# Attention scores as two float32r products over stacked 128-row operands, in a two-block transformer step on one core

## The chip, the cores and the metric

The kernel runs on one core of one Trainium2 chip. The metric is device time in microseconds of one execution; the times given are of several runs, of which the median counts. Lower is better. One execution was also taken by the profiler, and the rows below are of that one.

## The reference, cut to what matters

The input is a sequence of 512 tokens with 1024 features. Block one is run first (two layers), then block two (two layers). A layer of block one normalises `x`, multiplies it by a large input matrix, and cuts the result into three mixers: a sliding-window attention, a forgetting attention and a state-space scan. The scores of both attentions are what changes:

```python
# sliding window: 8 query heads, 2 key heads, head size 64, blocks of 128 queries
scores = jnp.einsum('bnqkgd,bnskd->bnkgqs', qb, kcat).astype(jnp.float32) * (hd ** -0.5)
...
# forgetting attention: 8 heads, head size 64, causal, with a bias from cumulated gates
logits = jnp.einsum('bqhd,bkhd->bhqk', qi, k).astype(jnp.float32) * scale
logits = logits + ci[..., :, None] - c[:, :, None, :]
```

In the sliding window each query block of 128 sees its own and the previous key block (256 keys; the first block has 128), and queries and keys carry rotary positions. In the forgetting attention query block i sees the i + 1 key blocks up to its own (128, 256, 384 or 512 keys). After softmax and the product with the values, each head is multiplied by a gate `silu(g)`, and everything goes through an output matrix and is added to `x`. The layer ends with an attention to a memory. All arrays are float32.

## The kernel before, in words

**Layout.** Activations lie with features on the 128 partitions and the 512 tokens along the free axis, eight tiles of 128 x 512. A Tile program with named pools is compiled to one instruction queue per engine; the order in each queue comes from a scheduler that puts earlier program lines first among what is ready, so work written later fills the waits of work written earlier, as far as buffers allow.

**Projections.** `steps` (L506; run to its end by `gemm`, L476) makes one feature tile of 128 x 512 after the other. Its weights come by `load` (L453): a 512 KB transfer on SP's queue, a float32r copy `wh` by ScalarE (L460), the remainder `wl` by VectorE (L462). The product is three float32r matmuls for each of eight blocks of 128 rows (`mm3`, L469 to L474: hi by hi, hi by lo, lo by hi), 24 matmuls in one PSUM buffer of the pool "g", which has two. Then a callback takes the tile out of PSUM. After every second tile `aside` (L494) lets in two steps of the modulation matmuls of block two (`adaln`, L1040), once `self.side` is set (L712).

**The mixer** `mixer1` (L563) runs once per layer. The feature tiles of its input matrix are numbered: 0 and 1 to 4 values of the two attentions, 5 the two rotary key heads, 6 to 9 the rotary queries, 10 to 13 gates of the sliding window, 14 to 17 keys and 18 to 21 queries of the forgetting attention, 22 to 25 its gates, 26 to 37 the convolution's input, 38 to 45 gates of the state-space part. The order written is:

1. Tiles 0 and 1 (values: copy, four transposes, copy; `cb_v`, L586), then 5 to 9 (`cb_rope`, L600: four ScalarE copies that swap quarters, two VectorE and one GpSimd operation), then 2 to 4 (L617 to L619).
2. The gates' small rows and their softplus chain (L620 to L665).
3. The sliding window (L672 to L710): for each of four head pairs j, each half of the queries and each head a of the pair, one block: a bfloat16 matmul writes the mask over 512 columns (L680), two score matmuls add the products (L685), VectorE takes the maximum (L688), ScalarE the exponentials (L694), VectorE scales them (L701). `weigh` (L995) transposes the probabilities (L1004), copies them (L1007) and multiplies by the values (L1010). The gate tile 10 + j is made inside the loop (L708).
4. Tiles 14, 18, 15, 19 and so on, kept by one copy each (`cb_keep`, L716 to L722), gates 22 to 25 (L724), and the first quarter of the output projection (L725).
5. The forgetting attention (L726 to L743): for head pair j, query block i and head a, one block: two bfloat16 matmuls for bias and triangle mask (L734, L735), the score matmul (L736), `softmax_rows` (L976), `weigh`, and at the pair's end the product with the gate (L742), which frees the one PSUM buffer of the pool "o".
6. Convolution tiles 26 to 37 (`cb_conv`, L750; L765), the state-space scan (L766 to L834), further parts of the output projection.

The score operands of before are plain float32 tiles; head a of a pair lies on partitions 64a to 64a + 63:

```python
ten.matmul(s3[:, i2, 256 - n:], qT[j][a * 64:a * 64 + 64, i * P:(i + 1) * P],
           kT[a * 64:a * 64 + 64, k0:k0 + n], start=False, stop=i2 == 1)
...
ten.matmul(s_, kq[2 * j + 1][a * 64:a * 64 + 64, i * P:(i + 1) * P],
           kq[2 * j][a * 64:a * 64 + 64, :n], start=False, stop=True)
```

They lie, with values, gates and convolution outputs, in the pool "f2", which has 24 tiles of 128 x 512.

Of the kernel before, what the change touches and what calls it, by code (L numbers as in the profile page):

```python
# [10 lines left out]
F32R = mybir.dt.float32r  # L11
# [4 lines left out]
AF = mybir.ActivationFunctionType  # L16
OP = mybir.AluOpType
# [3 lines left out]
P = 128  # L21
# [213 lines left out]
class _K:  # L235
# [306 lines left out]
    def hilo(self, src, tag):  # L542
# [2 lines left out]
        self.nc.vector.tensor_tensor(lo, src, hi, OP.subtract)  # L545
        return hi, lo

    def tokens(self, src, nt, dst):

        pp = self.pt("t")[:, :nt * P]  # L550
        for i in range(nt):
            self.nc.tensor.transpose(pp[:, i * P:(i + 1) * P], src[:, i * P:(i + 1) * P], self.idf)
        self.nc.scalar.activation(dst, pp.rearrange("p (i d) -> p i d", i=nt), AF.Copy)
# [9 lines left out]
    def mixer1(self, l, x, ps, rb):  # L563
        nc = self.nc
        A = self.A
        ten, vec, act, pool = nc.tensor, nc.vector, nc.scalar, nc.gpsimd
        wf = A[f"w_f{l}"]
# [15 lines left out]
        hT = self.norm(x, 4, self.v(f"nmix{l}"), keep=small, rb=rb, ps=ps)  # L583
# [14 lines left out]
        qk = []  # L598

        def cb_rope(f, s, ps):  # L600
            sw = self.tl("tg", [P, 512])
            for b in range(4):
                act.activation(sw[b * 32:(b + 1) * 32], ps[(b ^ 1) * 32:(b ^ 1) * 32 + 32], AF.Copy)
            o = self.tl("f2", [P, 512])
            vec.tensor_tensor(o, ps, rope, OP.mult)
            pool.tensor_tensor(sw, sw, rops, OP.mult)
            vec.tensor_tensor(o, o, sw, OP.add)
            qk.append(o)

        def cb_gate(lst):  # L610
            def cb(f, s, ps):
                o = self.tl("f2", [P, 512])
                self.gate(ps, o)
                lst.append(o)
            return cb

        self.gemm(wf, range(2), [hT], cb_v, 1, 2)  # L617
        self.gemm(wf, range(5, 10), [hT], cb_rope)
        self.gemm(wf, range(2, 5), [hT], cb_v)  # L619
        zt = self.tl("tg", [P, 512])  # L620
        act.activation(zt, pz, AF.Copy)
        pp = self.pt("t")
# [43 lines left out]
        kT, qT = qk[0], qk[1:5]  # L666
# [5 lines left out]
        for j in range(4):  # L672
            po = self.pt("o")
            for ip in range(2):
                p2 = []
                for a in range(2):
                    hh = 2 * j + a
                    s_ = self.pt("s")
                    s3 = s_.rearrange("p (i n) -> p i n", i=2)
                    ten.matmul(s_, self.idb, self.bandb if ip else self.band0b, start=True, stop=False)  # L680
                    for i2 in range(2):
                        i = 2 * ip + i2
                        k0 = max(i - 1, 0) * P
                        n = 256 if i else P
                        ten.matmul(s3[:, i2, 256 - n:], qT[j][a * 64:a * 64 + 64, i * P:(i + 1) * P],  # L685
                                   kT[a * 64:a * 64 + 64, k0:k0 + n], start=False, stop=i2 == 1)
                    m = self.sm("mx", [P, 2])
                    vec.tensor_reduce(m, s3, AX.X, OP.max)  # L688
                    nmx = self.sm("nmx", [P, 2])
                    vec.tensor_scalar(nmx, m, -0.125, nsink[:, hh:hh + 1], OP.mult, OP.min)  # L690
                    p3 = self.tl("t", [P, 2, 256])
                    den = self.sm("den", [P, 4])
                    for i2 in range(2):
                        act.activation(p3[:, i2], s3[:, i2], AF.Exp, bias=nmx[:, i2:i2 + 1], scale=0.125,  # L694
                                       accum_out=den[:, i2:i2 + 1])
                    act.activation(den[:, 2:4], nmx, AF.Exp, bias=self.v(f"sink{l}")[:, hh:hh + 1])
                    vec.tensor_tensor(den[:, :2], den[:, :2], den[:, 2:4], OP.add)
                    rd = self.sm("rd", [P, 2])
                    vec.reciprocal(rd, den[:, :2])
                    for i2 in range(2):  # L700
                        vec.tensor_scalar(p3[:, i2], p3[:, i2], rd[:, i2:i2 + 1], None, OP.mult)  # L701
                    p2.append(p3)
                for i2 in range(2):
                    i = 2 * ip + i2
                    self.weigh(po[:, i * P:(i + 1) * P], [p[:, i2] for p in p2],
                               [(b * P, va[:, i - 1 + b]) for b in range(0 if i else 1, 2)])
            y = self.tl("t", [P, 512])
            self.gemm(wf, [10 + j], [hT], cb_gate(ga))  # L708
            vec.scalar_tensor_tensor(y, po, 0.5, ga[j], OP.mult, OP.mult)
            y0.append(self.hilo(y, "y"))  # L710
# [3 lines left out]
        kq = []  # L714

        def cb_keep(f, s, ps):  # L716
            o = self.tl("f2", [P, 512])
            act.activation(o, ps, AF.Copy)
            kq.append(o)

        for j in range(4):
            self.gemm(wf, [14 + j, 18 + j], [hT], cb_keep)  # L722
        gb, y1 = [], []
        self.gemm(wf, range(22, 26), [hT], cb_gate(gb))  # L724
        self.gemm(A[f"w_o{l}0"], range(4), [y0], self.add_to(x), 2)  # L725
        for j in range(4):  # L726
            po = self.pt("o")
            for i in range(4):
                n = (i + 1) * P
                ss = []  # L730
                for a in range(2):
                    h = 2 * j + a
                    s_ = self.pt("s")[:, :n]
                    ten.matmul(s_, self.selb[:, h:h + 1].to_broadcast([72, P]), rows[:, :n], start=True, stop=False)  # L734
                    ten.matmul(s_[:, i * P:], self.idb, self.causb, start=False, stop=False)  # L735
                    ten.matmul(s_, kq[2 * j + 1][a * 64:a * 64 + 64, i * P:(i + 1) * P],  # L736
                               kq[2 * j][a * 64:a * 64 + 64, :n], start=False, stop=True)
                    ss.append(s_)
                pr_ = self.softmax_rows(ss, n, 0.125)
                self.weigh(po[:, i * P:(i + 1) * P], pr_, [(kt * P, vb[j][:, kt]) for kt in range(i + 1)])  # L740
            y = self.tl("t", [P, 512])
            vec.scalar_tensor_tensor(y, po, 0.5, gb[j], OP.mult, OP.mult)  # L742
            y1.append(self.hilo(y, "y"))  # L743
# [24 lines left out]
        for g in range(2):  # L768
# [4 lines left out]
            for c in range(4):  # L773
# [3 lines left out]
                o = self.tl("f2", [P, 8, 64])  # L777
# [4 lines left out]
            for c in range(4):  # L782
# [7 lines left out]
                for hf in range(2):  # L790
                    pa = self.pt("s").rearrange("p (h l) -> p h l", h=4)
                    for hh in range(4):
                        h = 8 + 8 * g + 4 * hf + hh
                        ten.matmul(pa[:, hh], self.selb[:, h:h + 1].to_broadcast([72, P]), rows[:, cs],
                                   start=hh == 0, stop=hh == 3)
# [14 lines left out]
                for ft in range(4):  # L810
                    for a in range(2):
                        hh = 2 * ft + a
                        o = py[a * 64:a * 64 + 64, ft]
# [3 lines left out]
                for ft in range(4):  # L817
                    f = 4 * g + ft
# [20 lines left out]
        for f in range(8):  # L839
# [3 lines left out]
            hi, lo = self.pair("h", 512)  # L843
# [1011 lines left out]
```

## Time and profile before

| | |
|---|---|
| median of 3 runs | 3039.6 us (3034.33 to 3042.72) |
| profiled execution | 3043.31 us |
| its span, first to last instruction | 3041.3 us |
| TensorE busy | 2846.7 us, 94% |
| VectorE busy | 1493.5 us, 49% |
| ScalarE busy | 1164.2 us, 38% |
| GpSimd busy | 267.0 us, 9% |
| mean granted clock of TensorE | 0.972 of full |

PE is TensorE's matmuls, PEld its weight loads, DVE is VectorE, ACT ScalarE, POOL GpSimd, SP the queue that issues most transfers. A name such as `pss<-f,f` says what is written and read: `pss` is the PSUM pool of the scores, `psg` that of the projections. A matmul's shape is given as rows * columns of its weights, then rows x columns of what streams through. float32 and float32r both stand as f32; float32r are L472 to L474. A float32 matmul stands as two instructions. Matmuls overlap, so their durations are longer than the distance from one start to the next; it is the starts that tell what a matmul costs.

### The profile page before, as it was taken

The numbers are of one execution on the slowest core, as the hardware profiler recorded it, in microseconds if no ns is written. First come the engines' busy times: TensorE is split into PE (matmuls) and PEld (weight loads), VectorE is DVE, ScalarE is ACT, GpSimd is POOL, SyncE is SP. The second block draws the span as 40 slices with busy tenths as digits, with TensorE's granted clock in tenths as the row PEclk, the third lists the DMA queues.
The fourth block names the chain that finished last, engine by engine and source line by source line (L and its number), as shares of the span: only waits on it lengthen the run. The fifth ranks groups of instructions, "written<-read, shape, count | busy, mean of one in ns | idle before, by whom it ended". The sixth has DMA issues, their size and how long they took to land. (4 is left out here: it accounts for less than half of the span.)

```text
span 3041.3 us, 46563 instructions
## 1 busy us (share of the span) xinstructions
PE 2846.7 (94%) x18975; PEld 1936.7 (64%) x18976; DVE 1493.5 (49%) x3051; ACT 1164.2 (38%) x2410; POOL 267.0 (9%) x256
## 2 busy tenths in 40 slices
PE   8999999999999999999989999989997999997975
PEld 5676667876777677887776788733334767774321
DVE  4625696544544687626355566631114365574100
ACT  4523454442542444434345343331112463443110
POOL 0000030000000011100011011011111010001101
PEclk9999999999999999999999999989997989997998
DMA  4142325421224134431111111489984111129998
GB/s 141 56 159 81 124 95 175 160 75 56 84 97 146 57 132 147 158 120 30 61 35 32 49 38 39 188 338 368 374 317 120 58 33 53 52 65 354 410 404 302
DMA packets 97573, 439.52 MB, mean 145 GB/s; under 512 B 11216, under 2 KB 12496, under 8 KB 72784
## 3 DMA queue, kind: packets, MB, share of 16 engines
q1 hardware_dynamic: 86976, 401.09, 36.4%
q0 software_dynamic: 9520, 32.32, 4.0%
q8 instruction: 149, 2.44, 0.3%
q10 hardware_dynamic: 864, 3.15, 0.3%
q14 instruction: 64, 0.52, 0.1%
HBM read 416.40 MB, written 20.97 MB: 144 GB/s over the span
## 5 line engine op out<-in xcount | busy, mean ns | idle before, releaser
L472 PE MATMUL psg<-h,wh 128*128 128x512 f32 x1616 | 654.1, 405 | 0.7 <-DVE x L1078 0.4
L473 PE MATMUL psg<-h,wh 128*128 128x512 f32 x1616 | 648.2, 401 | 0.0
L474 PE MATMUL psg<-h,wl 128*128 128x512 f32 x1616 | 647.2, 401 | 0.0
L462 DVE TENSOR_TENSOR wl<-wr,wh 128x1024 fp32r<-128x1024 f32 (+2 forms) x272 | 338.9, 1247 | 493.9 <-ACT wh L460 482.1
L460 ACT ACTIVATE wh<-wr 128x1024 fp32r<-128x1024 f32 (+2 forms) x272 | 280.9, 1033 | 608.6 <-PE psg L473 536.0
L472 PEld LDWEIGHTS psg<-h,wh 128*128 128x128 f32 x1616 | 305.2, 189 | 94.8 <-issue 24.6
L473 PEld LDWEIGHTS psg<-h,wh 128*128 128x128 f32 x1616 | 305.2, 189 | 75.1 <-issue 14.2
L474 PEld LDWEIGHTS psg<-h,wl 128*128 128x128 f32 x1616 | 305.5, 189 | 73.8 <-issue 12.4
L1727 PE MATMUL psg<-ew,xg 128*64 128x512 f32 x832 | 222.7, 609 | 23.8 <-DMA ew<-in_eu_dram 13.1
L472 PE MATMUL psg<-y,wh 128*128 128x256 f32 (+1 forms) x560 | 181.1, 324 | 1.5 <-ACT y L448 0.8
L473 PE MATMUL psg<-y,wh 128*128 128x256 f32 (+1 forms) x560 | 180.5, 323 | 1.9 <-DVE y L449 1.9
L474 PE MATMUL psg<-y,wl 128*128 128x256 f32 (+1 forms) x560 | 178.9, 321 | 0.0
L1727 PEld LDWEIGHTS psg<-ew,xg 128*64 128x64 f32 x832 | 65.3, 139 | 156.3 <-issue 113.6
L472 PE MATMUL psg<-f,wh 128*128 128x256 f32 (+1 forms) x360 | 115.1, 321 | 4.1 <-DVE x L557 1.8
L1007 ACT ACTIVATE t<-pst 128x512 f32<-128x512 f32 (+1 forms) x134 | 70.0, 557 | 127.6 <-PE pst L1004 124.6
L472 PEld LDWEIGHTS psg<-y,wh 128*128 128x128 f32 x560 | 107.9, 193 | 14.8 <-DVE x L1078 2.1
L473 PE MATMUL psg<-f,wh 128*128 128x256 f32 (+1 forms) x360 | 114.3, 318 | 0.8 <-DVE f L1242 0.8
L473 PEld LDWEIGHTS psg<-y,wh 128*128 128x128 f32 x560 | 107.5, 193 | 11.5 <-DVE y L449 2.2
L474 PE MATMUL psg<-f,wl 128*128 128x256 f32 (+1 forms) x360 | 113.0, 314 | 0.0
L474 PEld LDWEIGHTS psg<-y,wl 128*128 128x128 f32 x560 | 107.9, 193 | 6.1 <-issue 0.6
L1754 PE MATMUL pss<-ew,hid 128*64 128x512 f32 x400 | 106.1, 597 | 2.8 <-DMA ew<-in_ed_dram 2.6
L1004 PE MATMUL pst<-const_sb,t 128*128 128x128 f32 x488 | 84.5, 284 | 4.5 <-DVE t L1232 3.3
(465 smaller groups left out, 4431.3 us busy)
## 6 DMA issues: line engine op xcount, KB each, us to landing
ew<-in_eg_dram SPq DMA_DIRECT2D x52, 1024.0 KB, 20.9
ew<-in_eu_dram SPq DMA_DIRECT2D x52, 1024.0 KB, 8.4
ew<-in_ed_dram SPq DMA_DIRECT2D x50, 1024.0 KB, 8.8
wm<-in_wm_dram SPq DMA_DIRECT2D x96, 512.0 KB, 3.8
wr<-in_w_f_dram SPq DMA_DIRECT2D x92, 512.0 KB, 3.5
wr<-in_v_f_dram SPq DMA_DIRECT2D x60, 512.0 KB, 3.3
wr<-in_w_o_dram SPq DMA_DIRECT2D x32, 512.0 KB, 3.5
x<-in_ed_dram SPq DMA_DIRECT2D x10, 1024.0 KB, 10.3
```

Source lines behind the costliest of these rows:

```text
L460: nc.scalar.activation(hi, raw, AF.Copy)
L462: nc.vector.tensor_tensor(lo, raw, hi, OP.subtract)
L472: t.matmul(ps, a[0], b[0], start=first, stop=False)
L473: t.matmul(ps, a[0], b[1], start=False, stop=False)
L474: t.matmul(ps, a[1], b[0], start=False, stop=last)
L1004: ten.transpose(pp[:, (2 * i + a) * P:(2 * i + a + 1) * P], ps[a][:, c:c + P], self.idf)
L1007: self.nc.scalar.activation(pT[:, :w], pp[:, :w], AF.Copy)
L1727: ten.matmul(ps[e * 64:(e + 1) * 64], x0[:, d, e * 64:(e + 1) * 64], wn[e][:, k], start=d == 0, stop=d == 7)
L1754: ten.matmul(ps[e * 64:(e + 1) * 64], hid[0, q][:, f, e * 64:(e + 1) * 64], w[j][e][:, f], start=f == 0, stop=f == 3)
```

## The change

Each score operand becomes a tile of 128 rows for one head. For a query it holds the float32r rounding of the head's 64 rows in one half and the remainder in the other; for a key there are two tiles, the rounding in both halves and the remainder in both halves. A score is then the sum of two float32r matmuls over 128 rows with the same query tile, one with each key tile. The rotary result goes to the pool "t" first. In the first part value and rotary tiles alternate. Half of the forgetting attention's key and query tiles (16, 20, 17, 21) and its four gates are projected inside the loop over head pairs, not ahead of it.

```diff
+    def stacked(self, src, double):
+        act, vec, pool = self.nc.scalar, self.nc.vector, self.nc.gpsimd
+        lo_, up_ = slice(0, 64), slice(64, 128)
+        if not double:
+            o = [self.tl("f2", [P, 512], F32R) for _ in range(2)]
+            for a, (m, n) in enumerate(((lo_, up_), (up_, lo_))):
+                act.activation(o[a][m], src[m], AF.Copy)
+                vec.tensor_tensor(o[a][n], src[m], o[a][m], OP.subtract)
+            return o
+        o = [[self.tl("f2", [P, 512], F32R) for _ in range(2)] for _ in range(2)]
+        for a, (m, n) in enumerate(((lo_, up_), (up_, lo_))):
+            hi, lo = o[a]
+            act.activation(hi[m], src[m], AF.Copy)
+            act.activation(hi[n], src[m], AF.Copy)
+            vec.tensor_tensor(lo[m], src[m], hi[m], OP.subtract)
+            pool.tensor_copy(lo[n], lo[m])
+        return o
+
+    def scores(self, ps, q, k, last):
+        self.nc.tensor.matmul(ps, q, k[0], start=False, stop=False)
+        self.nc.tensor.matmul(ps, q, k[1], start=False, stop=last)
...
-            o = self.tl("f2", [P, 512])
+            o = self.tl("t", [P, 512])
...
-            qk.append(o)
+            qk.append(self.stacked(o, not qk))
...
-        self.gemm(wf, range(5, 10), [hT], cb_rope)
-        self.gemm(wf, range(2, 5), [hT], cb_v)
+        self.gemm(wf, (5, 2, 6, 3, 7, 4, 8, 9), [hT], lambda f, *a: (cb_v if f < 5 else cb_rope)(f, *a))
...
-                        ten.matmul(s3[:, i2, 256 - n:], qT[j][a * 64:a * 64 + 64, i * P:(i + 1) * P],
-                                   kT[a * 64:a * 64 + 64, k0:k0 + n], start=False, stop=i2 == 1)
+                        self.scores(s3[:, i2, 256 - n:], qT[j][a][:, i * P:(i + 1) * P],
+                                    [k[:, k0:k0 + n] for k in kT[a]], i2 == 1)
...
         def cb_keep(f, s, ps):
-            o = self.tl("f2", [P, 512])
-            act.activation(o, ps, AF.Copy)
-            kq.append(o)
-
-        for j in range(4):
+            kq.append(self.stacked(ps, f < 18))
+
+        gb, y1 = [], []
+        for j in range(2):
             self.gemm(wf, [14 + j, 18 + j], [hT], cb_keep)
-        gb, y1 = [], []
-        self.gemm(wf, range(22, 26), [hT], cb_gate(gb))
         self.gemm(A[f"w_o{l}0"], range(4), [y0], self.add_to(x), 2)
...
-                    ten.matmul(s_, kq[2 * j + 1][a * 64:a * 64 + 64, i * P:(i + 1) * P],
-                               kq[2 * j][a * 64:a * 64 + 64, :n], start=False, stop=True)
+                    self.scores(s_, kq[2 * j + 1][a][:, i * P:(i + 1) * P], [k[:, :n] for k in kq[2 * j][a]], True)
...
+            if j < 2:
+                self.gemm(wf, [16 + j, 20 + j], [hT], cb_keep)
+            self.gemm(wf, [22 + j], [hT], cb_gate(gb))
             y = self.tl("t", [P, 512])
             vec.scalar_tensor_tensor(y, po, 0.5, gb[j], OP.mult, OP.mult)
```

## Rows read from the trace of the kernel before

**Rows 1.** The page, busy us (share of the span), instructions.

```profile
PE 2846.7 (94%) x18975; PEld 1936.7 (64%) x18976; DVE 1493.5 (49%) x3051; ACT 1164.2 (38%) x2410; POOL 267.0 (9%) x256
```

**Rows 2.** Busy time by stretch; last PEclk, DMA share, GB/s.

```profile
91.00:159.00 68.00, 67.85 (x397) 44.52 (x398) 46.47 (x145) 38.86 (x117) 0.00 (x0) 1.00 0.13 40
159.00:250.00 91.00, 91.00 (x475) 69.53 (x470) 25.67 (x27) 20.82 (x26) 0.00 (x0) 1.00 0.52 177
250.00:340.00 90.00, 90.00 (x511) 54.62 (x510) 56.90 (x135) 42.93 (x108) 0.51 (x5) 1.00 0.12 37
...
340.00:385.00 45.00, 44.44 (x259) 30.71 (x260) 29.81 (x46) 14.53 (x20) 0.61 (x6) 1.00 0.61 211
385.00:456.00 71.00, 66.93 (x517) 48.42 (x516) 66.99 (x134) 41.88 (x110) 24.91 (x19) 1.00 0.25 83
...
806.00:874.00 68.00, 67.85 (x389) 44.91 (x388) 46.38 (x144) 38.69 (x116) 0.00 (x0) 1.00 0.13 40
```

**Rows 3.** Waits of PEld, 43 to 456 us: total us, times, longest.

```profile
PEld pso L1010 <- ACT t L1007: 9.8, 24, 0.8
...
PEld psg L472 <- ACT wh L460: 2.5, 6, 0.4
```

**Rows 4.** Timeline of PE, two sliding-window blocks: start us, us, then the instruction.

```profile
96.94 0.39 PE L680 MATMUL pss<-cstb 128*128 128x512 bf16 x1
...
98.31 0.50 PE L473 MATMUL psg<-h,wh 128*128 128x512 f32 x1
98.65 0.40 PE L474 MATMUL psg<-h,wl 128*128 128x512 f32 x1
...
113.25 0.38 PE L680 MATMUL pss<-cstb 128*128 128x512 bf16 x1
...
114.40 0.50 PE L472 MATMUL psg<-h,wh 128*128 128x512 f32 x1
```

**Rows 5.** Timeline of PE, three blocks of the forgetting attention.

```profile
269.85 0.22 PE L735 MATMUL pss<-cstb 128*128 128x128 bf16 x1
270.00 0.49 PE L736 MATMUL pss<-f,f 64*128 64x128 f32 x2
270.42 0.50 PE L473 MATMUL psg<-h,wh 128*128 128x512 f32 x1
...
285.78 0.22 PE L735 MATMUL pss<-cstb 128*128 128x128 bf16 x1
285.93 1.12 PE L736 MATMUL pss<-f,f 64*128 64x512 f32 x2
286.98 0.39 PE L734 MATMUL pss<-rows,cstb 72*128 72x512 bf16 x1
...
296.95 0.22 PE L735 MATMUL pss<-cstb 128*128 128x128 bf16 x1
...
297.73 0.28 PE L734 MATMUL pss<-rows,cstb 72*128 72x256 bf16 x1
```

**Rows 6.** Timeline of PE, float32r projections of 512 and 256 columns.

```profile
40.01 0.39 PE L472 MATMUL psg<-h,wh 128*128 128x512 f32 x1
...
40.46 0.39 PE L474 MATMUL psg<-h,wl 128*128 128x512 f32 x1
...
560.00 0.28 PE L473 MATMUL psg<-f,wh 128*128 128x256 f32 x1
...
560.60 0.28 PE L472 MATMUL psg<-f,wh 128*128 128x256 f32 x1
```

**Rows 7.** Single lines: instructions, duration in ns min/median/max, first and last start.

```profile
L718 ACT ACTIVATE f<-psg x16: 577/582/603, 157.9 to 915.8; 128x512 f32<-128x512 f32 x16
L605 DVE TENSOR_TENSOR f<-psg,f x10: 691/692/692, 55.0 to 791.7; 128x512 f32<-128x512 f32 x10
L460 ACT ACTIVATE wh<-wr x272: 630/1059/1082, 16.9 to 2743.3; 128x1024 fp32r<-128x1024 f32 x124, 128x768 fp32r<-128x768 f32 x8, 128x512 fp32r<-128x512 f32 x4
L462 DVE TENSOR_TENSOR wl<-wr,wh x272: 682/1226/2350, 19.0 to 2744.2; 128x1024 fp32r<-128x1024 f32 x124, 128x768 fp32r<-128x768 f32 x8, 128x512 fp32r<-128x512 f32 x4
```

## What the change should do to the time

> **What bounds the kernel now.** I read first the engines' shares, then the busy times by stage, then what TensorE waits for, then the order of its instructions. TensorE is busy for 94% of the span [rows 1]. The changed code lies in the token mixer of block one, which runs once per layer. In layer 0 its stretches are the sliding-window attention (91 to 159 us), the key, query and gate projections with the first part of the output projection (159 to 250), the forgetting attention (250 to 340), the rest of the convolution projections (340 to 385) and the state-space part (385 to 456). In the first four TensorE is busy for all but 0.7 us of 294, at the full granted clock; VectorE is busy for 46.5 of 68, 25.7 of 91, 56.9 of 90 and 29.8 of 45, ScalarE for less. Only in the fifth is VectorE nearly full (67.0 of 71) [rows 2]. Layer 1 repeats this: its sliding-window stretch has the same 68 us to a tenth [rows 2]. So up to the state-space part a microsecond less of TensorE work is a microsecond less of time, as long as other matmuls are ready. They are: the instructions of a projection stand between those of the attention, one or a few at a time [rows 4, 5], so the scheduler fills the softmax's latency with projections. The waits say the same: in the 413 us from 43 to 456 TensorE's weight loads waited 2.5 us for the split weights and 9.8 us, in 24 waits, for the copies of transposed probabilities [rows 3].
>
> **What the scores cost.** A score product of before reads float32 tiles over 64 rows and is run as two passes. In the sliding window a block is one 512-column mask matmul (L680) and two products. With two of 256 columns it takes from 96.94 to 98.31, 1.37 us; the float32r projection matmul behind it needs 0.34 to its successor (98.31 to 98.65) where such matmuls otherwise follow each other at 0.225 (40.01 to 40.46 in two steps), so the change of shape costs another 0.11. With products of 128 and 256 columns it is 113.25 to 114.40, 1.15 us and the 0.11 [rows 4, 6]. In the forgetting attention, from the start of the triangle mask (L735) to the instruction behind the product: 1.20 us for 512 columns, 0.78 for 256, 0.57 for 128 [rows 5]; 384 columns lie midway between the first two, 0.99.
>
> **What they will cost.** The new product is two float32r matmuls over 128 rows (the float32 operand's rounded part in one half, its remainder in the other; the keys' rounded part twice, then their remainder twice). That is the form of the projections, which follow each other at 0.225 us for 512 columns and 0.12 for 256 (560.00 to 560.60 in five steps) [rows 6]; 384 columns midway, 0.173. No float32r matmul of 128 columns stands in the trace. It can hardly cost more than a float32 pass of 128 columns, 0.21 (270.00 to 270.42 for two) [rows 5], nor less than half of 0.12; I take 0.12, the nearest row of the same kind, since a narrower matmul should not take longer than a wider one. Before the first float32r matmul of a block I leave the 0.15 us that now pass between mask and product (285.78 to 285.93) [rows 5]; at best it is 0.06.
>
> The sums, per layer:
> Sliding window, 8 blocks of 256 and 256: 1.37 + 0.11 now, 0.225 + 4 x 0.12 = 0.705 after, 0.775 less each, 6.2 us. 8 blocks of 128 and 256: 1.15 + 0.11 now, 0.705 after, 0.555 each, 4.4 us.
> Forgetting attention, 8 blocks of each width: 512: 1.20 - (0.15 + 0.45) = 0.60; 384: 0.99 - 0.50 = 0.49; 256: 0.78 - 0.39 = 0.39; 128: 0.57 - 0.39 = 0.18; together 1.66 x 8 = 13.3 us, and the 0.11 behind every second of the 32 blocks (the others are followed by a mask, without it), 1.8 us.
> 25.7 us per layer, **51 us** for both. Ends: with 0.21 for the 32 products of 128 columns per layer 2.9 us per layer are lost, 46 in all; with 0.06 for them, and 0.06 instead of 0.15 ahead of the 32 blocks of the forgetting attention, 4.8 us per layer are won, 61.
>
> **A rule against it.** The float32r stream has each matmul with a weight load of its own, all over the same 128 rows, and yet runs at 0.225 and 0.12, so the loads are hidden behind the matmuls before [rows 6]. The Trainium skill, "TensorE: Matmul & The Clock Gate", Part 3, says that a weight load overlaps with matmuls in flight only when the row group differs; by it the old products (rows 0 to 63, then 64 to 127) would be the ones that overlap, and the new ones would not. Here the trace speaks against the rule as far as this goes: it is the 64-row product that is followed by 0.34 instead of 0.225 [rows 4].
>
> **What is added.** In ScalarE: a key tile has four half-tile copies, a query tile two; L718's plain copy goes. Per layer 4 + 8 in the rotary projections, 16 + 8 - 8 in the others: 28 copies of 512 columns at 0.58, 16 us. VectorE: two subtractions per tile, 26 per layer at 0.69, 18 us [rows 7]. GpSimd: ten half-tile copies per layer; nothing waits for them but a key tile's scores, and GpSimd does nothing in the forgetting attention's 90 us but 0.5 us [rows 2]. All of it lies beside projections: a projection tile takes TensorE 24 x 0.225 = 5.4 us, and a key tile of the second kind needs ScalarE 4 x 0.58 and 1.06 for the next weights (3.4), VectorE 2 x 0.69 and 1.23 (2.6) [rows 7]. A rotary key tile needs ScalarE for four shifted copies as well (5.7 us), over 5.4, but there is one per layer, and the new order puts value tiles between, which need 1.2 and the weights. If that cover is gone, the price is the 34 us per layer themselves. A PSUM buffer of the projections (there are two) is held for some 3 us in place of 0.6; the next tile writes the other for 5.4.
>
> **What is moved.** The order of value and rotary tiles changes no work; the value transposes stay. Key and query tiles 16, 20, 17, 21 and the gates 22 to 25, eight tiles or 43.5 us of TensorE, go from the stretch ahead of the forgetting attention into it, with their weight loads on SP's queue and the modulation matmuls that every second tile lets in. They become the fill that five of the convolution tiles are now, and these go behind; TensorE's sum is the same. The pool of 24 float tiles makes this order necessary: 4 values, 12 for two pairs, 6 for the next and a gate are 23, so convolution outputs cannot be made early. New wait: in a head pair j the product of output and gate (L742) comes after gate 22 + j, and the one PSUM buffer of the output is free only then; behind it wait the next pair's value matmuls on TensorE, while projections are ready. I cost it at nothing: the gate tile itself fills the time. VectorE in the sliding-window stretch: 46.5 us in 68 - 10.6 = 57.4, 81%; still under TensorE.
>
> For stalls that show when TensorE is quicker I take 5 us of the 51 back (a quarter of the 9.8 us of [rows 3] in each layer, an estimate). So 46 us less. The profiled execution has 3043.3 us (span 3041.3), 3.7 over the median of 3039.6; 46 from the median gives 2994.
>
> **Rivals.**
> A. *The softmax sets the sliding window's length.* VectorE has the softplus chain there too, its queue is in order, and 81% may be full in practice. Then that stretch keeps its 68 us and its 10.6 us per layer are lost: 51 - 5 - 21 = 25 less, 3015. For it: VectorE has the highest share of the first four stretches there. Against: TensorE can take key and query tiles from the stretch behind, where VectorE has 25.7 of 91 [rows 2].
> B. *Weight loads no longer hidden*, as a mechanism of these products: each of the 128 products per layer pays its load of 0.19 us, 24 of the 25.7 us, and 3 us in all are left, 3036: no change. That is what the skill's rule above would give. Against: the stream at 0.12.
> C. *The stacking becomes the bound, slower.* Copies and subtractions stand in the same in-order queues as the weight split (L460, L462) and the exponentials; once a tile's work there passes TensorE's 5.4 us, TensorE waits for split weights. All 34 us exposed against 25.7 won: 8 us per layer, 3056. It decides from the point where key tiles fall among exponentials in the forgetting attention, ScalarE 42.9 of 90 now. Against: there ScalarE has 47 and VectorE 33 of 90 us free, and five convolution tiles with four VectorE sweeps each leave it.
> D. *The products do not run as single passes*, but as the float32 ones do. Then the second product doubles the scores' passes (sliding window 16 blocks at 1.37 or 1.15 less the mask and its wait, 0.30 to 0.32, 15 us; forgetting the four widths' times less 0.15, together 2.94, by 8, 24 us), 39 us per layer, 3118. Against: the projections have the same type.
>
> **How the numbers follow.** Forecast 0.70, A 0.14, B 0.04, C 0.06, D 0.02; 0.04 is left for mixtures between A and no change. A measurement of this kernel tells 0.3%, 9 us, from no change. Forecast and A are faster, with half of the rest: 0.86; B and the other half the same: 0.06; C and D slower: 0.08. The range goes from 61 us less (2978) to A with 5 us more of stalls (3020); the forecast alone would be 2978 to 2999.
>
> **What would show it.** Right: blocks with L680 at about 0.7 us, the 512-column forgetting product 0.45 in two matmuls, no 0.34 behind; sliding-window and forgetting stretches still without TensorE idle time, everything behind them earlier by 21 to 28 us per layer; the state-space part's 71 us unchanged. Wrong: TensorE waiting for L460, L462 or for the key copies (C), VectorE near 100% from 91 to 150 us with TensorE waiting there for the scalings of L701 or the copies of L1007 (A), 0.3 us between 256-column products (B).

## The result, and the profile after

| | before | after |
|---|---|---|
| median of four runs | 3039.2 us (3034.3 to 3042.7) | 3013.4 us (3010.2 to 3019.4) |
| ratio to before | | 0.992 (0.9907 to 0.9934) |
| once more, beside the last experiments | 3038.7 | 3011.8, 0.9915 (0.9902 to 0.9929) |
| profiled execution, its span | 3043.3, 3041.3 | 3010.2, 3007.3 |
| last state-space chunk of layer 1 begins (L787, after: L810) | 1154.1 | 1124.9 |

The change makes the kernel 26 us faster; 46 were forecast. The last row of the table is where block one's changed part ends in the trace (the last start of the line, before and after):

```profile
L787 ACT ACTIVATE t<-pss x16: 255/277/278, 385.5 to 1154.1; 128x128 f32<-128x128 f32 x16
L810 ACT ACTIVATE t<-pss x16: 252/277/280, 369.2 to 1124.9; 128x128 f32<-128x128 f32 x16
```

It leaves out what follows, which took 1876 to 1887 us in the kernels below with the same code. By it the change gives 29 us, 16 in layer 0 and 13 in layer 1. It is used below beside the timed ratios. But it is read from one execution: a second one of the changed kernel has 1124.3, and 0.9 us less in layer 0, so differences of about 1 us say nothing.

The busy time by stretch, layer 0 of the changed kernel, with columns as in [rows 2] (window, its length, then PE, PEld, DVE, ACT and POOL busy, granted clock, DMA share, GB/s); the sliding window now ends at 167 us, the forgetting attention runs from 202 to 300, the state-space part from 369:

```profile
43.00:91.00 48.00, 42.49 (x195) 34.24 (x194) 18.08 (x20) 25.91 (x38) 5.09 (x5) 1.00 0.28 88
91.00:128.00 37.00, 34.12 (x190) 26.50 (x189) 27.22 (x75) 22.98 (x54) 2.57 (x2) 1.00 0.24 71
128.00:167.00 39.00, 38.76 (x268) 27.92 (x267) 29.79 (x85) 27.58 (x82) 1.22 (x2) 1.00 0.18 61
...
202.00:300.00 98.00, 97.52 (x650) 70.00 (x650) 54.48 (x125) 49.55 (x118) 2.45 (x4) 1.00 0.27 92
300.00:369.00 69.00, 69.00 (x377) 53.13 (x376) 52.25 (x76) 25.06 (x36) 1.11 (x11) 1.00 0.51 176
369.00:440.00 71.00, 66.83 (x514) 48.26 (x513) 67.26 (x135) 41.59 (x109) 24.34 (x19) 1.00 0.24 83
```

From 128 us on TensorE stands still for 0.7 us up to the state-space part, which keeps its 71 us. But from 43 to 128 us it is idle for 8.4 of 85 us. Before, the same two stretches were

```profile
43.00:91.00 48.00, 47.22 (x218) 38.37 (x218) 17.96 (x19) 25.85 (x38) 6.47 (x5) 1.00 0.33 99
91.00:128.00 37.00, 36.85 (x200) 24.20 (x198) 26.32 (x86) 20.41 (x61) 0.00 (x0) 1.00 0.14 43
```

with 0.9 us idle. So the first part of the mixer, where projections run almost alone, and the begin of the sliding window lost 7.5 us of what the attentions won. The waits of PE, 43 to 385 us, in the changed kernel (columns as in [rows 3]):

```profile
PE pst L577 <- ACT tg L613: 5.5, 4, 1.7
PE pst L648 <- ACT tg L645: 2.5, 1, 2.5
```

L577 are the transposes of a value tile (L552 before), L613 the ScalarE copy that they read; L648 transposes the gates' small rows, whose copy is L645. Before, these waits were 0.8 us in all:

```profile
PE pst L552 <- ACT tg L588: 0.8, 1, 0.8
```

The timeline shows how they come about, first all engines, 57 to 61 us:

```profile
57.56 0.63 ACT L562 ACTIVATE f<-t 64x512 fp32r<-64x512 f32 x1 [2.13 <-DVE t L632]
58.21 0.63 ACT L563 ACTIVATE f<-t 64x512 fp32r<-64x512 f32 x1
...
58.86 0.63 ACT L562 ACTIVATE f<-t 64x512 fp32r<-64x512 f32 x1
...
59.51 0.63 ACT L563 ACTIVATE f<-t 64x512 fp32r<-64x512 f32 x1
...
60.16 0.60 ACT L613 ACTIVATE tg<-psg 128x512 f32<-128x512 f32 x1
...
60.81 0.66 PE L577 MATMUL pst<-const_sb,tg 128*128 128x128 f32 x4 [1.70 <-ACT tg L613]
```

ScalarE has made the key tile's four shifted copies, waits 2.13 us for the sum of the rotation (product on VectorE, product on GpSimd, sum on VectorE), then makes the four stacking copies; the value tile's copy is the next in its queue. TensorE's last projection matmul had begun at 58.72; the transposes are its next instruction, and the projections behind them start only after them.

The score blocks, sliding window and forgetting attention of 512 columns (L704 is the mask, L570 and L571 the two products, L755 and L756 bias and triangle):

```profile
103.65 0.39 PE L704 MATMUL pss<-cstb 128*128 128x512 bf16 x1
...
104.11 0.28 PE L570 MATMUL pss<-f,f 128*128 128x256 f32 x1
104.23 0.28 PE L571 MATMUL pss<-f,f 128*128 128x256 f32 x1
104.34 0.40 PE L472 MATMUL psg<-h,wh 128*128 128x512 f32 x1
104.58 0.39 PE L473 MATMUL psg<-h,wh 128*128 128x512 f32 x1
...
242.48 0.22 PE L756 MATMUL pss<-cstb 128*128 128x128 bf16 x1
242.51 0.48 PE L570 MATMUL pss<-f,f 128*128 128x512 f32 x1
242.82 0.40 PE L571 MATMUL pss<-f,f 128*128 128x512 f32 x1
243.06 0.39 PE L755 MATMUL pss<-rows,cstb 72*128 72x512 bf16 x1
```

The first block takes 0.69 us where 1.37 stood [rows 4], the second 0.58 where 1.20 stood [rows 5], and the projection behind follows at 0.24, not 0.34.

### The profile page after: what moved, and what is told of

Its sections match the earlier page's. It is cut to its first block, busy times and chain, and to the rows that moved or that the text cites. A ratio compares the mean times of both kernels' runs of the same rounds, so it can differ in the third digit from the quotient of the medians.

```text
span 3007.3 us, 46731 instructions
## 1 busy us (share of the span) xinstructions
PE 2794.3 (93%) x18975; PEld 1932.1 (64%) x18976; DVE 1532.0 (51%) x3103; ACT 1198.2 (40%) x2466; POOL 278.6 (9%) x276
```

## The experiments

Medians with the ratio to the kernel before and its 95% interval; the third column of numbers is the begin of layer 1's last state-space chunk in the trace.

| kernel | median, us | ratio | chunk, us | at half clock |
|---|---|---|---|---|
| before | 3036.4 to 3039.2 | | 1154.1 | 0 |
| changed | 3013.4, 3011.8 | 0.992, 0.9915 | 1124.9, 1124.3 | 1, 1 |
| old order of tiles | 3008.8 | 0.9901 (0.9887 to 0.9915) | 1122.3 | 3 |
| new order alone | 3039.3 | 1.0006 (0.9996 to 1.0016) | 1154.5 | 0 |
| one product | 2985.6 | 0.9833 (0.9817 to 0.9849) | 1102.5 | 1 |
| value copy on VectorE | 3011.2 | 0.9903 (0.9887 to 0.9919) | 1123.9 | 2 |
| move alone | 3033.7 | 0.9991 (0.9981 to 1.0000) | 1146.7 | 2 |
| rotary stacking on GpSimd | 3003.4 | 0.9884 (0.9866 to 0.9902) | 1117.9 | 1 |
| the same, old order | 3001.1 | 0.9893 (0.9876 to 0.9909) | 1114.8 | 3 |
| keep copies twice | 3014.2 | 0.9922 (0.9904 to 0.9940) | 1127.0 | 2 |
| early gates | 3007.7 | 0.9896 (0.9882 to 0.9911) | 1121.5 | 1 |
| early gates, GpSimd | 3001.6 | 0.9879 (0.9863 to 0.9894) | 1118.1 | 2 |
| early gates, GpSimd, old order | 3001.0 | 0.9877 (0.9862 to 0.9892) | 1112.4 | 1 |

The traces differ in the granted clock too. Each has a stretch of 6.8 us at half the clock where layer 1 begins. The last column of the table counts the further stretches of 3.4 us at half the clock up to the last chunk (in the move alone and keep copies twice, one of the two lengthens the stretch at the begin of layer 1). In most of them TensorE is busy throughout, so such a one costs some 1.7 us, an estimate. The three of the old order:

```profile
84.80:88.20 3.40, 3.40 (x11) 2.80 (x10) 0.36 (x1) 0.60 (x1) 0.00 (x0) 0.51 0.56 154
784.60:788.00 3.40, 3.40 (x9) 2.67 (x8) 0.00 (x0) 0.13 (x1) 0.00 (x0) 0.50 0.53 154
1112.30:1115.70 3.40, 3.40 (x14) 2.02 (x14) 3.40 (x4) 0.28 (x1) 1.09 (x1) 0.50 0.40 149
```

**The order of the tiles undone.** The theory: the transposes wait because value tiles now stand between rotary ones.

```diff
-        self.gemm(wf, (5, 2, 6, 3, 7, 4, 8, 9), [hT], lambda f, *a: (cb_v if f < 5 else cb_rope)(f, *a))
+        self.gemm(wf, range(5, 10), [hT], cb_rope)
+        self.gemm(wf, range(2, 5), [hT], cb_v)
```

> The changed kernel with the first part's tiles in the old order (key and queries 5 to 9 in a row, then values 2 to 4), all else as changed. Theory: the missing 8 us per layer are TensorE's waits for value transposes and for the gates' small transposes, whose ScalarE copies stand behind the rotary and stacking copies in ScalarE's queue; then 14 us come back, 2999 us (2994 to 3004), and the waits of the value transposes fall from some 8 us per layer to under 2. Rival: with stacking, rotary tiles in a row keep ScalarE busy for 4.6 to 5.7 us of each 5.4 and hold PSUM, so TensorE waits in another place and the time stays at 3010 to 3016. Second rival: the loss is in the sliding window, which VectorE sets; then the order is worth under 4 us.

Only 2.6 us came back by the trace, and the intervals of the two ratios overlap. Two more stretches at half the clock than in the changed kernel, an estimated 3.4 us, may hide as much again. The waits of PE, 43 to 300 us, and the busy time from 43 to 167:

```profile
PE pst L577 <- ACT tg L613: 3.6, 3, 2.5
PE psg L472 <- DVE t L630: 2.7, 3, 1.2
```

```profile
43.00:167.00 124.00, 118.03 (x656) 90.56 (x654) 75.30 (x180) 74.72 (x172) 9.31 (x9) 0.99 0.25 77
```

TensorE is idle for 6.0 us instead of 8.6. The small transposes' wait is gone and the value transposes still wait 3.6 us, not under 2; a new wait stands there: projections wait for a PSUM buffer until VectorE's rotary product (L630) has read it. So the order makes a part of the loss, not the whole of it. What the trace shows is the rival's mechanism, though the time, 3008.8, lies just below the rival's 3010 to 3016.

**The new order alone**, in the kernel before (the same lines the other way round).

> The kernel before with the alternating order of value and rotary tiles alone. Theory: without stacking ScalarE has 2.4 us of rotary copies per tile, not 4.7 to 5.0, so a value tile's copy waits less; 2 to 6 us slower than before (3041 to 3046), since four shifted copies still stand ahead of each. Rival (the order is free by itself, the waits come from stacking alone): within 2 us of before.

No difference, 0.4 us in the trace; the forecast loss of 2 to 6 us did not come. Without stacking the alternation costs nothing, so the waits need the stacking copies.

**The value copy on VectorE.**

```diff
         def cb_v(f, s, ps):
             t = self.tl("tg", [P, 512])
-            act.activation(t, ps, AF.Copy)
+            vec.tensor_copy(t, ps)
```

> The changed kernel with the value tiles' copy out of PSUM on VectorE in place of ScalarE; the order of tiles is the changed one. If ScalarE's queue is what the value transposes wait for, their waits shrink from 6 us per layer to under 2 and 8 to 12 us come back (3001 to 3005 us); the gates' small transposes keep their 2.5 us per layer. If it is the pool of the copies' tiles (three, shared with the rotary part) that holds them, the waits stay and so does the time (3010 to 3016).

```profile
PE pst L577 <- DVE tg L613: 3.5, 3, 1.2
PE pst L648 <- ACT tg L645: 2.5, 1, 2.5
```

The waits fell from 5.5 to 3.5 us, not to under 2: VectorE's queue in turn holds the copy behind rotary sums and remainders. By the trace 1.0 us is won, no more than two executions of one kernel differ by; one more stretch at half the clock, an estimated 1.7 us, hides some of it. So one copy out of ScalarE's queue is not enough.

**The rotary stacking's rounded copies on GpSimd**, which has little else to do there.

```diff
+    def stacked(self, src, double, pooled=False):
...
-                act.activation(o[a][m], src[m], AF.Copy)
+                (pool.tensor_copy(o[a][m], src[m]) if pooled else act.activation(o[a][m], src[m], AF.Copy))
...
-            act.activation(hi[m], src[m], AF.Copy)
-            act.activation(hi[n], src[m], AF.Copy)
+            (pool.tensor_copy(hi[m], src[m]) if pooled else act.activation(hi[m], src[m], AF.Copy))
+            (pool.tensor_copy(hi[n], src[m]) if pooled else act.activation(hi[n], src[m], AF.Copy))
...
-            qk.append(self.stacked(o, not qk))
+            qk.append(self.stacked(o, not qk, True))
```

> The changed kernel with the rounded copies of the rotary operands made by GpSimd in place of ScalarE (12 half-tile copies per layer; order of tiles as changed, the other key and query tiles as changed). Theory: ScalarE's in-order queue is what the value transposes and the gates' small transposes wait for, and its load in the first part falls back to that of before: TensorE's idle time from 43 to 167 us falls from 8.6 us to 2 to 3, and 10 to 14 us come back in both layers, 2999 to 3003 us. Rival: it is the length of the rotary chain itself (VectorE, GpSimd, VectorE, copies) with two PSUM buffers, and GpSimd's 0.6 us copies after its 1.3 us product only lengthen it: 3010 us or more.

> The same with the tiles in the old order (5 to 9, then 2 to 4). If ScalarE's queue is the cause, the order is then worth little: 2998 to 3004 us, within 4 us of the run with GpSimd copies in the alternating order, and TensorE waits under 1 us for PSUM buffers held by the rotary product. If rotary tiles in a row are too much for the two PSUM buffers whoever copies, it stays at 3007 to 3011, where the old order alone was.

Busy time by stretch with GpSimd's copies, new order:

```profile
43.00:91.00 48.00, 47.22 (x216) 38.23 (x215) 20.29 (x22) 24.42 (x35) 14.02 (x14) 1.00 0.31 94
91.00:128.00 37.00, 33.59 (x192) 25.80 (x191) 30.46 (x86) 19.31 (x52) 5.36 (x6) 1.00 0.20 65
```

From 43 to 91 us TensorE is as full as before the change: 0.8 us idle where the changed kernel has 5.5. The wait for the value copies is 0.8 us. This is the test that settles the cause there: same order, same tiles, same stacking, only the rounded copies gone from ScalarE. What is not won back stands at the begin of the sliding window, 3.4 us in 91 to 128, now as waits for exponentials and the small rows:

```profile
PE pss L704 <- ACT t L718: 2.2, 2, 1.6
PE pst L648 <- ACT tg L645: 1.0, 1, 1.0
```

All in all 7.0 us by the trace, with as many stretches at half the clock, and 0.992 or 0.9915 against 0.9884 by the times. That is less than forecast: TensorE is idle for 4.4 us from 43 to 167, not 2 to 3, and 10 to 14 us were to come back. The old order with it gives 10.1 us by the trace, in spite of two more stretches at half the clock, and times that can't be told from these; with rotary tiles in a row there are still 2.2 us of waiting for PSUM from 43 to 167, where under 1 was expected.

**The gates' small rows and softplus chain ahead of the rotary and value tiles**: L644 to L690 of the changed kernel placed behind the first two value tiles; once with ScalarE's copies, twice with GpSimd's.

> The changed kernel with the gates' small rows and softplus chain ahead of the rotary and value tiles, ScalarE's rotary copies kept. It takes away the wait of the small transposes alone (2.5 us per layer, and in layer 1 the 3.4 us at half clock behind it, worth 1.7): 4 to 8 us less than the changed kernel, 3005 to 3010; the value transposes' waits stay at some 5.5 us per layer. If the lost time is all in the value transposes' waits: no change (within 3 us).

> The kernel with GpSimd's rotary copies (alternating order), and the gates' small rows with their softplus chain written ahead of the rotary and value tiles, not behind them. Theory: the copy that the small transposes wait for then stands ahead of the rotary copies, and some 12 us of VectorE's short operations leave the sliding window; TensorE's idle time from 43 to 167 us falls from 4.4 us to about 2, 3 to 8 us less than the run with GpSimd copies alone (2995 to 3000). Rival: the chain's own transposes and products now stop the projections while they wait for VectorE, and nothing is won (3001 to 3006).

> The same with tiles 5 to 9 in a row and 2 to 4 behind them. By the theory within 4 us of the alternating order, 2995 to 3002. If rotary tiles in a row hold PSUM too long beside the softplus chain on VectorE, 5 us or more above it.

> The changed kernel itself once more, to have it beside these on one chip: 3008 to 3016 us, 0.990 to 0.994 of before.

With ScalarE's copies 3.4 us by the trace are won (0.9896 against 0.9915, intervals overlapping): a little under the forecast. The small transposes no longer wait, but the first masks do (L704 for VectorE's L714, 2.1 us), and layer 1 keeps its 3.4 us at half the clock, from 801.8 us on; the value transposes wait 3.8 us, where 5.5 were expected to stay. With GpSimd's copies nothing is seen to be won in the new order (1118.1 against 1117.9, with one more stretch at half the clock), the rival's case. TensorE's idle time from 43 to 167 us does not fall from 4.4 to 2 but rises to 6.3, in other waits:

```profile
PE pss L704 <- ACT t L718: 2.9, 1, 2.9
PE pst L686 <- DVE parts L683: 1.1, 1, 1.1
PE pst L667 <- issue: 1.0, 1, 1.0
```

In the old order 2.4 us are won by the trace, less than the estimated 3.4 us of the two stretches at half the clock that this trace has fewer, so no gain of the early gates is shown. Of all kernels this one has the earliest chunk among those that compute everything, 12 us before the changed kernel's; by the times it is 0.9877 of before, 0.996 of the changed kernel, and not told apart from the other three with GpSimd's copies.

**One product** (the second matmul of `scores` taken out).

> The changed kernel without the second score product (the part of the scores that comes from the keys' remainder is left out). It takes TensorE work out and nothing else: per layer 24 products of 256 and 8 of 128 columns in the sliding window, 8 of each width in the forgetting attention, 3.4 and 4.6 us, 16 us for both layers. Theory, TensorE sets the time of both attentions: 13 to 17 us under the changed kernel, 2997 us. Rival, the softmax on VectorE and ScalarE sets the sliding window's length after the change: at most the forgetting attention's 9 us come, 3004 or more.

22.4 us less by the trace, 25 to 28 by the times (0.9833 against 0.9915 and 0.992; medians 2985.6 and 3013.4): more than the 16 forecast, since the second product takes 10.9 us of TensorE per layer (the sum of start-to-start distances of the score matmuls falls from 24.4 to 13.5 us), not 8. In layer 0 the chunks begin 11.8 us earlier. TensorE's work in the attentions is paid one for one: the softmax does not set the sliding window's length.

**The move alone**, in the kernel before: its `cb_keep` with one copy, tiles 16, 20, 17, 21 and 22 to 25 in the loop.

> The kernel before with the move alone: key and query tiles 16, 20, 17, 21 and the gates 22 to 25 projected inside the loop of the forgetting attention, operands and scores as before. Theory: TensorE's sum is the same and projections are ready either way, so within 3 us of before (3036 to 3042). Rival: convolution tiles that fill the attention now come behind it, where VectorE has less room, and 5 to 10 us are lost; or the new place lets more be filled and 5 to 10 are won.

The time is 2.7 us less, inside what was expected, with an interval from 0 to 5.8 us; the trace has 7.4 us, 6.6 of them in layer 0. So the move costs nothing and wins at most a few microseconds. In the trace of layer 0 the projections and modulation matmuls stand more often among their own kind; whether that is the reason was not followed up. Layer 1 has only 0.8 us of it; against it stand 6.8 us more at half the clock than before the change, an estimated 3.4 us at most.

**Keep copies twice**: in the forgetting attention's `stacked`, each ScalarE copy is issued two times.

> The changed kernel with each ScalarE copy of the forgetting attention's key and query stacking made twice (24 more copies of some 0.6 us per layer, 14 us; the result is the same). Theory: there the added work lies beside projections and costs nothing: within 3 us of the changed kernel (3010 to 3016). Rival: part of the unpaid gain is given back there too, by PSUM buffers held longer and exponentials put off; then 6 to 28 us more (3019 and up).

```profile
167.00:300.00 133.00, 132.29 (x820) 95.68 (x819) 69.65 (x143) 70.05 (x148) 3.67 (x6) 1.00 0.34 111
```

ScalarE is busy for 70.1 of these 133 us (58.7 in the changed kernel), TensorE is idle for 0.7, and the time is that of the changed kernel (in the trace 2.1 us more, with 3.4 us more at half the clock at the begin of layer 1). There the stacking is covered with room to spare.

## Why the prediction was right or wrong

**The bound** was read rightly: where attention and projections run side by side, TensorE stays full after the change, and what is taken from it is taken from the time (one product, keep copies twice).

**The range** held, but not for the reason forecast: 3013.4 us lies outside 2978 to 2999, where the forecast alone put it, and inside only because the range reached to rival A. That it came out beside A's 3015 is luck.

**The sum for the scores** was right in its mechanism, a little large. For layer 0, from 43 us to the first state-space chunk, I added up the distances from each TensorE matmul's start to the next. Scores and the three bias and mask lines go from 51.4 to 30.8 us. Transposes of probabilities go from 14.4 to 12.8; only 10 of the 136 stood directly behind a 64-row product, so most of this stays unexplained. The projections go from 237.1 to 242.9: 7.6 us more before value and small transposes, 1.8 less elsewhere, which is found behind the score products: 22 projections there cost 3.0 us over 0.225 each before, 20 cost 1.0 after. 20.6 + 1.6 + 1.8 is 24.0 us of the 25.7 predicted.

The prices of the blocks after were good (0.69 for 0.705, 0.58 for 0.60), but not their parts: the first product starts 0.03 to 0.04 us after the mask, where 0.225 and 0.15 were taken, and its second follows after 0.30 to 0.31, where 0.12 and 0.225 were taken. The two errors cancel, which is luck. The prices before were a little high, 48.5 us without the changes of shape where 46.7 are measured, for a reason not followed up. The move was put at nothing; alone, in the kernel before, it won 6.6 us in layer 0, some 5 of them in closer projections. In the changed kernel the projections that do not wait are only 1.8 us closer, and that stands behind the scores; why the two gains do not add is open.

**The step that failed** is the sentence that the added copies lie beside projections, with the one about the order of tiles: "the new order puts value tiles between, which need 1.2 and the weights". That compared ScalarE's work per tile with TensorE's 5.4 us and found it smaller. In the trace it is smaller: ScalarE is busy for 25.9 of the 48 us. But the copy that TensorE waits for stands behind a chain in an in-order queue, with ScalarE idle for 2.1 us in the middle of it. 7.6 us were lost so in layer 0, and the same four waits stand in layer 1, where I had put 2.5 per layer for all stalls. Stalls were expected in the attentions, with a quarter of [rows 3]; there hardly any came (0.7 us from 128 us on). Rival C named this mechanism, copies ahead of others in ScalarE's queue, but placed it in the forgetting attention and on the weight split, where it does not occur.

**Layer 1** lost more. There TensorE's wait for the small rows was followed by a stretch at a lower clock:

```profile
797.79 0.39 PE L474 MATMUL psg<-h,wl 128*128 128x512 f32 x1
800.70 0.84 PE L648 MATMUL pst<-const_sb,tg 128*128 128x128 f32 x4 [2.52 <-ACT tg L645]
...
801.77 0.63 PE L473 MATMUL psg<-h,wh 128*128 128x512 f32 x1
802.19 0.63 PE L474 MATMUL psg<-h,wl 128*128 128x512 f32 x1
```

```profile
801.00:804.50 3.50, 3.50 (x14) 2.70 (x13) 2.10 (x8) 2.43 (x8) 0.38 (x1) 0.51 0.31 124
```

For 3.5 us the granted clock is 0.51 of full, the level of 1.2 GHz, and projections follow each other at 0.42 us, not 0.225. That is some 1.7 us, half of the 3.4 us that layer 1 won less than layer 0; the other half was not followed up. The same stop of 2.91 us in layer 0, from the projection at 99.54 to the small transposes at 102.45, was followed by no fall of the clock.

**Rival A** gave 3015, where the time came out, but its mechanism is not what happened: from 128 to 167 us TensorE is full with VectorE at 29.8 of 39, and taking TensorE work out of the sliding window still shortens it. **Rival B** fell: the products of 128 rows follow each other at 0.12 (104.11 to 104.23 to 104.34), though each has a weight load of 0.19 us, so the loads are hidden. The rule of the Trainium skill ("TensorE: Matmul & The Clock Gate", Part 3) that the prediction set beside it, that a weight load overlaps with matmuls in flight only when the row group differs, is not borne out by this trace. **D** fell with the same rows. Stretches behind were to be earlier by 21 to 28 us per layer; they were by 16 and 13. The state-space part's 71 us came true.

What stays open: from 43 to 167 us of layer 0 TensorE was idle for 0.9 us before the change and still for 4.4, 3.5, 6.3 and 4.4 us in the four kernels with GpSimd's copies (in the order of the table), in waits that move from one place to another, some before the sliding window and some at its begin. Keeping ScalarE and VectorE clear of every rotary operation there was not tried.

## What to carry to other kernels

Work added to an engine with time to spare is free only if nothing that the bounding engine waits for stands behind it in the same queue: look in the trace at what is next in that queue, and at the chain that the added work itself waits for, before comparing sums. When a stall is found, ask whether it is the order of the work or the queue it is in; here the old order moved part of the wait to another place, and an idle engine for the copies took about half of the idle time away (8.6 to 4.4 us). A float32 product over 64 rows is worth rewriting as two float32r products over 128 where the projections around it have that form: here a pass of 256 columns fell from 0.22 us to 0.12, and most of the price of the change of shape behind it went. When two traces differ by a few microseconds, compare their granted clocks before giving the change the credit.

## What was not expected of the hardware

A float32r matmul of 128 columns, of which the trace before had none, is cheap: in blocks with no wait the first of a pair is followed by the second after 0.06 us and that by the next after 0.11.

```profile
96.80 0.22 PE L570 MATMUL pss<-f,f 128*128 128x128 f32 x1
96.86 0.28 PE L571 MATMUL pss<-f,f 128*128 128x128 f32 x1
96.97 0.33 PE L570 MATMUL pss<-f,f 128*128 128x256 f32 x1
```

So the price lies at or below the 0.12 that was taken, far from the 0.21 of a float32 pass. And the clock's fall in layer 1 came after a stop of under 3 us, from the start of the last projection at 797.79 to 800.70, while a stop of the same length in layer 0 was followed by none. Both executions of the changed kernel show this.
